# An encoder block on one core: a third seven-product K pair in the output projection, transposed halves in another sequence, token sums at other steps

## The chip, the cores and the metric

The kernel runs on one core of one Trainium2 chip. A core has five engines that run at once, each with its own in-order queue: TensorE (PE in the profile; PEld is its weight load), VectorE (DVE), ScalarE (ACT), GpSimd (POOL) and SyncE (SP), which here issues the loads. They share an on-chip memory (SBUF) and the accumulators of TensorE (PSUM). The metric is device time in microseconds from one launch, median of the runs; lower is better.

## The reference, cut to what matters

One layer of an encoder block in float32, 256 tokens of width 2048. What is computed:

```python
h = rms_norm(x, g_mix); proj = h @ w_in        # q, k, v of three mixers, and three gates
oa, ob, oc = mixer_a(...), mixer_b(...), mixer_c(..., mem)   # dilated windows, grouped-query, cross-attention
gates = sigmoid(gt).reshape(b, s, 3, D_MODEL)
merged = gates[:, :, 0] * (oa @ w_br_a) + gates[:, :, 1] * (ob @ w_br_b) + gates[:, :, 2] * (oc @ w_br_c)
x = x + merged @ w_o                           # "the projection" below
hf = rms_norm(x, g_ffn) @ w_ffn_in             # 2048 -> 2 x 5632
x = x + (silu(hf[..., :D_FF]) * hf[..., D_FF:]) @ w_ffn_out
```

## The kernel before, in words

**Split operands.** Each float32 operand is split into a high half, rounded by ScalarE (`whi` for weights, L397), and a low half, the rest, by VectorE (`wlo`, L407). A product of 128 rows by 512 columns is then three matmuls: high x high, high x low, low x high.

**Pairs and steps.** From the merging stage on, all matrix products run as pairs: two blocks of 512 output columns (c = 0, 1), two blocks of 128 tokens (t = 0, 1), and K in pairs of 128-row blocks (K pair u is blocks 2u and 2u+1). A whole K pair takes 8 products: step `d`u for column block 0 and step `D`u for column block 1, four products each, into the PSUM banks Y, V and Z, Q. A K pair can instead take seven products of summed operands, as Strassen and Winograd do: step `f`u (banks X, Y), step `g`u (W, Z), `h` (V, for up to two K pairs), `p` and `q` (X, for up to two K pairs each). Its weight sums are VectorE adds (L506, L507, L513, L529) and one transfer that adds while it loads, issued by POOL (L485); its token sums ("forms") are made by `token_sums` (L796 to L798 and a split, L130 and L131) from a full operand that VectorE (L807) or ScalarE (L301) puts together. The lists `STEPS_*` (L54 to L61) say in which order the steps of a pair run. In the projection's list two of the eight K pairs take seven products, in the first FFN list three, in the later ones four.

**What sets the order.** `run` keeps five steps in flight: a step's loads, sums and splits are written when it is reached, its matmuls four steps later. TensorE and SyncE keep the program's order; the weight splits and sums keep it among themselves (`follow`), and a low half is written one step after its high half (`low(1)`). Everything else on VectorE and ScalarE is placed by the compiler's planner, with `high_priority` for what is marked urgent. Each step that has been multiplied is a tick; `side` holds jobs that wait for a tick, and one of them advances at each tick. A number that a job yields is how many ticks it waits.

**Around the change.** When a column block of the projection ends, `add` adds it to the residual (L872), and its job `later` squares it (L878), waits 2 ticks, and calls `transposed`: two halves, two ticks apart, each with four transposes by TensorE into one PSUM bank, then a split with the gain into `x1T` (L133 on ScalarE, L134 on VectorE), which the FFN multiplies. For four of the eight halves ScalarE also copies the rows for the forms (L301). When an FFN pair ends, VectorE multiplies its two blocks (L924), and the result is transposed into `hT`, the operand of the output stage (`feeding`). There are three rounds of FFN pairs (four, four, three) and output pairs (two each); the last round's output lists are `STEPS_LAST` and `STEPS_LAST2`. At the head of each output stage `sums_of` makes one form from `hT`; it lies in a buffer of its own, `form`.

The times are those of the profile's execution: the projection's matmuls run from 580 to 670 us.

Of the kernel before, what the change touches and what calls it, by code (L numbers as in the profile page):

```python
# [11 lines left out]
F32 = mybir.dt.float32  # L12
F32R = mybir.dt.float32r
I32 = mybir.dt.int32
AF = mybir.ActivationFunctionType
ALU = mybir.AluOpType
# [3 lines left out]
S = 256  # L20
# [32 lines left out]

STEPS_GATE = "d4 d0 D0 f1 g1 d5 D5 f2 d6 g2 D4 f3 h1 g3 p0 p2 D6 q0 h3 q2 d7 D7".split()  # L54
STEPS_IN = "d0 D0 f1 d5 D5 g1 f2 g2 d6 h1 f3 f4 g3 D6 g4 p0 p2 h3 q0 q2 d7 D7".split()
STEPS_O = "d0 D0 d1 D1 f2 d4 g2 D4 f3 d5 g3 D5 h2 d6 p0 D6 q0 d7 D7".split()
STEPS_FFN = "d0 D0 d1 D1 f2 f3 d5 g2 D5 g3 h2 f4 d6 g4 p0 p2 h4 D6 q0 q2 d7 D7".split()
STEPS_OUT = "d3 d2 d1 f5 d0 D2 D1 f6 D0 g5 f7 D3 g6 g7 p0 p2 h5 q0 q2 h7 d4 D4".split()
STEPS_OUT2 = "d1 d2 d0 f5 D0 D2 g5 f6 f7 g6 g7 p0 d3 p2 D1 h5 h7 q0 D3 q2 d4 D4".split()
STEPS_LAST = "d1 d0 D0 D1 f2 g2 d4 D4 f3 g3 p0 h2 q0 d5 D5".split()  # L60
# [41 lines left out]
def encoder_block(ctx: ExitStack, tc: tile.TileContext, a: dict, out: bass.AP):  # L102
    nc = InOrder(tc)
# [16 lines left out]
    def s4(shape, name, dt=F32):  # L120
        return mid.tile(shape, dt, name=name, tag="s4")

    def bank(name, tag="at"):
        return psum.tile([P, NC], F32, name=name, tag=tag)


    def split(hi, lo, src, scale=None):

        if scale is None:
            nc.scalar.activation(hi, src, AF.Copy)  # L130
            nc.vector.tensor_sub(lo, src, hi.bitcast(F32))  # L131
        else:
            nc.scalar.activation(hi, src, AF.Copy, scale=scale)  # L133
            nc.vector.scalar_tensor_tensor(lo, src, scale, hi.bitcast(F32), op0=ALU.mult, op1=ALU.subtract)  # L134
# [145 lines left out]
    def transposed(src, dst, g=None, lag=1, also=None):  # L280


        for h in range(2):
            if h:
                yield lag
            tp = bank("tp", "mm" if h and nc.on else "at")
            for k in range(2):
                for t in range(T):
                    nc.tensor.transpose(tp[:, k * S + t * P:k * S + (t + 1) * P],
                                        src[t][:, (2 * h + k) * P:(2 * h + k + 1) * P], ident)  # L290
            if g is None:
                d = dst(2 * h, 2)
                split(d[0], d[1], tp.rearrange("p (k s) -> p k s", s=S))
            else:
                for k in range(2):
                    d = dst(2 * h + k, 1)
                    split(d[0], d[1], tp[:, k * S:(k + 1) * S], g(2 * h + k))
            if also and also(h):
                full = s4([P, 4, P], "ffull")
                for k in range(2):  # L300
                    nc.scalar.activation(full[:, 2 * k:2 * k + 2], tp[:, k * S:(k + 1) * S].rearrange(  # L301
                        "p (b s) -> p b s", s=P), AF.Copy, scale=g(2 * h + k) if g else 1.0)
                also(h)(full)
# [485 lines left out]
    mT, x1T, x = [], [], []  # L789
# [8 lines left out]
        nc.vector.tensor_add(raw[:, 3], raw[:, 2], full[:, 2])  # L798
        split(to[:, 0], to[:, 1], raw)

    def sums_of(lhs, these, room):

        def steps():
            for u, to in zip(these, room):
                full = s4([P, 4, P], "ffull")
                for k in range(2):
                    nc.vector.tensor_add(full[:, 2 * k:2 * k + 2].rearrange("p t s -> p (t s)"),  # L807
                                         *(v.bitcast(F32) for v in lhs(2 * u + k)))
                token_sums(full, to)
                yield 1  # L810
        start(steps())
        return by_pair(these, room)

    def by_pair(these, room):
        return lambda u, f: (room[these.index(u)][:, 0, (f + 1) % 4], room[these.index(u)][:, 1, (f + 1) % 4])

    def form_room(n, pool=None):
        tiles = [s8([P, 2, 2, 4, P], "forms", pool=pool) for _ in range((n + 1) // 2)]
        return [tiles[i // 2][:, i % 2] for i in range(2 * len(tiles))]

    form = lambda: spare[0].tile([P, 2, 4, P], F32R, name="form")

    def merging():
        forms = sums_of(xT, (1, 2, 3, 4), form_room(4, tail))
        for b, (g0, k0, k1) in enumerate(((0, 0, 2), (8, 2, 6), (4, 6, 12))):
            for j in (0, 2) if b else (2,):
                sg = [None, None]

                def gates(c, r, sg=sg):
                    sg[c] = r  # L830
                    for t in range(T):
                        nc.scalar.activation(r[:, t], r[:, t], AF.Sigmoid, scale=r_x[:, 0, t:t + 1])

                def merge(c, r, j=j, b=b, sg=sg):
                    n0 = (j + c) * NC
                    for t in range(T):
                        nc.vector.tensor_mul(sg[c][:, t] if b else mg[t][:, n0:n0 + NC], r[t], sg[c][:, t])

                    def later():
                        yield 1  # L840
                        for t in range(T):
                            m = mg[t][:, n0:n0 + NC]
                            nc.vector.tensor_add(m, m, sg[c][:, t])
                        if b == 2:
                            to = s8([P, 2, 4, S], "mT", pool=tail)
                            mT.append(to)
                            yield 2
                            yield from transposed([mg[t][:, n0:n0 + NC] for t in range(T)],
                                                  lambda k, n: (to[:, 0, k:k + n], to[:, 1, k:k + n]))
                    if b:  # L850
                        start(urgent(later()))

                yield pair(block_pair(a["w_gate"], g0 + j), xT, STEPS_IN if b else STEPS_GATE, gates, forms)
                yield pair(lambda u, c, j=j, k0=k0: a["w_br"][j + c][k0 // PK + u], lambda k, k0=k0: ol(k0 + k),
                           whole_k((k1 - k0) // 2), merge)

    x1l = lambda k: (x1T[k // 4][:, 0, k % 4], x1T[k // 4][:, 1, k % 4])
    forms, room = [], []


    def projecting():
        x.extend(s8([P, D], f"x{t}", F32) for t in range(T))
        for t in range(T):
            nc.sync.dma_start(out=x[t], in_=a["x"][t * P:(t + 1) * P, :])
        x1T.extend(s8([P, 2, 4, S], "x1T") for _ in range(4))
        mTl = lambda k: (mT[k // 4][:, 0, k % 4], mT[k // 4][:, 1, k % 4])
        oforms = sums_of(mTl, (2, 3), form_room(2))
        for n in (0, 2):
            def add(c, r, n=n):
                xc = [x[t][:, (n + c) * NC:(n + c + 1) * NC] for t in range(T)]  # L870
                for t in range(T):
                    nc.vector.tensor_add(xc[t], r[:, t], xc[t])  # L872

                def later():
                    yield 1
                    sq = s4([P, T, NC], "sq")
                    for t in range(T):
                        nc.scalar.activation(sq[:, t], xc[t], AF.Square, accum_out=ss1[:, t, n + c:n + c + 1])  # L878
                    yield 2
                    if n + c == 0:  # L880
                        room.extend(form_room(4) + [form()])
                        forms.append(by_pair((1, 2, 3, 4), room[:4]))

                    def token_forms(h):
                        u = 2 * (n + c) + h
                        return (lambda v: token_sums(v, room[u - 1])) if 1 <= u <= 4 else None
                    yield from transposed(xc, lambda k, m: (x1T[n + c][:, 0, k], x1T[n + c][:, 1, k]),
                                          lambda k: gT[:, 2, 4 * (n + c) + k:4 * (n + c) + k + 1], 2,
                                          also=token_forms)
                    if n + c == 3:  # L890
                        yield 2
                        ssr = small.tile([P, T], F32, name="ss", bufs=1)
                        nc.vector.tensor_reduce(ssr, ss1, axis=AX.X, op=ALU.add)
                        row_scale(ssr, r_f)
                start(urgent(later()))
            yield pair(block_pair(a["w_o"], n), mTl, STEPS_O, add, oforms)

# [5 lines left out]
    def feeding():  # L903
        for c0, c1 in ((0, 4), (4, 8), (8, KF // 4)):
            hT = []
            last = c1 == KF // 4
            hTl = lambda k, hT=hT: (hT[k // 4][:, 0, k % 4], hT[k // 4][:, 1, k % 4])
# [23 lines left out]
                           lambda u, f: forms[0](u, f))  # L931
            if last:
                pairs = STEPS_LAST, STEPS_LAST2
                sums_of(hTl, (1,), room[4:])
                out_forms = by_pair((1, 2, 3), room[4:] + late)
            else:
                pairs = STEPS_OUT, STEPS_OUT2
                sums_of(hTl, (5,), room[4:])
                out_forms = by_pair((5, 6, 7), room[4:] + late)
            for n in (0, 2):  # L940
                def output(c, r, n=n, last=last):
# [108 lines left out]
```

## Time and profile before

| What | Value |
|---|---|
| median of the runs | 1368.85 us |
| the profiled execution | 1369.74 us |
| its span, first to last instruction | 1368.0 us |
| instructions in all | 17866 |
| VectorE busy | 1190.5 us (87%) |
| ScalarE busy | 865.4 us (63%) |
| moved between HBM and the core | 298.86 MB |

TensorE's busy time is modelled from pipelined matmuls, so a busy TensorE may still hold short waits; they show in the start times of matmuls that follow each other. The profiled execution is one run; numbers of single instructions are its own, and its time is 0.89 us above the median.

### The profile page before, as it was taken

The page shows a single profiled execution, that of the slowest core. Times are in us where ns is not written, and L with a number is a line of the kernel's source. Part 1 is how long each engine was busy: PE and PEld are TensorE (multiplying, and loading weights), DVE is VectorE, ACT ScalarE, POOL GpSimd, SP SyncE. Part 2 cuts the span into 40 slices and gives each one's busy share as a digit, 9 for nine tenths or more (in the row PEclk, how much of TensorE's full clock was granted, in tenths as well). Part 3 has the DMA queues.
Part 4 walks back from the last instruction along what each step waited for, and adds up shares of the span by engine and source line. Part 5 has one row for each costly group of instructions (what it writes and reads, how often), then busy time and mean ns, then how long its engine had stood idle before and what let it go on. Part 6 is the DMA issues. An engine that isn't in the chain of part 4 may idle for free.

```text
span 1368.0 us, 17866 instructions
## 1 busy us (share of the span) xinstructions
PE 1358.7 (99%) x6195; PEld 1125.7 (82%) x6195; DVE 1190.5 (87%) x1652; ACT 865.4 (63%) x1152; POOL 85.1 (6%) x97
## 2 busy tenths in 40 slices
PE   9999999999999999999999999999999999999998
PEld 7888888888888888887878888888888888888887
DVE  6868877759889888878999998989999989899998
ACT  7777665646665565656776666655666765566754
POOL 0010000000000100000000010000001000011000
PEclk9999999999999999999999999999999999999999
DMA  9976445557776775954777777777787767787673
GB/s 366 343 234 203 151 156 168 171 166 225 239 237 201 225 242 180 308 181 146 242 223 220 233 211 221 220 246 212 222 247 218 230 187 243 217 247 225 204 224 108
DMA packets 91674, 298.86 MB, mean 218 GB/s; under 512 B 10368, under 2 KB 12928, under 8 KB 91328
## 3 DMA queue, kind: packets, MB, share of 16 engines
q1 hardware_dynamic: 79488, 275.94, 60.2%
q0 software_dynamic: 11952, 21.76, 9.7%
q8 instruction: 48, 0.79, 0.2%
q14 instruction: 42, 0.34, 0.1%
q10 hardware_dynamic: 144, 0.02, 0.0%
HBM read 294.81 MB, written 2.88 MB: 218 GB/s over the span
## 4 chain that ended last, share of the span: by engine, by line
PE 86%; DVE 8%; issue 2%; DMA 2%; ACT 1%; SPq 0%; DVEq 0%; ACTq 0%
PE mm L77 16%; PE mmZ L77 14%; PE mmV L77 14%; PE mmY L77 14%; PE mmQ L77 11%; PE mmX L77 10%; DVE wlo L407 4%; PE mmW L77 3%; DMA raw<-in_w_ffn 2%; PE tp L77 1%; ACT whi L397 1%; PE sc L77 1%; PE o L77 1%; DVE t L506 1%; PE pT L77 1%
## 5 line engine op out<-in xcount | busy, mean ns | idle before, releaser
L397 ACT ACTIVATE whi<-raw 128x1024 fp32r<-128x1024 f32 (+1 forms) x460 | 479.4, 1051 | 350.6 <-PE mmV L77 109.6
L407 DVE TENSOR_TENSOR wlo<-raw,whi 128x1024 fp32r<-128x1024 f32 (+1 forms) x460 | 546.8, 1210 | 80.7 <-ACT whi L397 77.5
L77 PE MATMUL mm<-whi,xT 128*128 128x512 f32 x640 | 202.5, 393 | 0.0
L131 DVE TENSOR_TENSOR wlo<-raw,whi 128x1024 fp32r<-128x1024 f32 x82 | 102.1, 1248 | 43.6 <-ACT whi L130 42.9
L77 PEld LDWEIGHTS mm<-whi,xT 128*128 128x128 f32 x640 | 119.3, 188 | 23.5 <-issue 0.4
L130 ACT ACTIVATE whi<-raw 128x1024 fp32r<-128x1024 f32 x82 | 86.7, 1061 | 62.3 <-PE mm L77 45.4
L77 PE MATMUL mm<-wlo,xT 128*128 128x512 f32 x320 | 125.7, 393 | 0.0
L407 DVE TENSOR_TENSOR wlo<-t,whi 128x1024 fp32r<-128x1024 f32 x90 | 102.2, 1138 | 13.4 <-ACT whi L397 12.9
L397 ACT ACTIVATE whi<-t 128x1024 fp32r<-128x1024 f32 x90 | 89.0, 990 | 25.5 <-PE mmQ L77 11.4
L77 PE MATMUL mmX<-whi,forms 128*128 128x512 f32 x312 | 104.9, 389 | 0.0
L77 PE MATMUL mmY<-whi,x1T 128*128 128x512 f32 x266 | 96.7, 394 | 0.8 <-DVE x1T L134 0.8
L77 PE MATMUL mmV<-whi,x1T 128*128 128x512 f32 x266 | 91.3, 390 | 0.0
L77 PEld LDWEIGHTS mm<-wlo,xT 128*128 128x128 f32 x320 | 60.2, 188 | 12.3 <-issue 0.7
L77 PEld LDWEIGHTS mmX<-whi,forms 128*128 128x128 f32 x312 | 58.6, 188 | 12.3 <-ACT SB L448 0.2
L485 POOL DMA_DIRECT2D raw<-in_w_ffn x43 | 37.2, 865 | 441.0 <-DMA raw<-in_w_ffn 143.3
L77 PE MATMUL mmZ<-whi,x1T 128*128 128x512 f32 x180 | 63.0, 391 | 0.0
L77 PE MATMUL mmQ<-whi,x1T 128*128 128x512 f32 x180 | 62.8, 390 | 0.0
L77 PE MATMUL mmW<-whi,forms 128*128 128x512 f32 x156 | 61.6, 395 | 0.0
L77 PE MATMUL mmZ<-whi,forms 128*128 128x512 f32 x156 | 60.9, 390 | 0.0
L77 PE MATMUL mmX<-wlo,forms 128*128 128x512 f32 x156 | 60.8, 389 | 0.0
L77 PEld LDWEIGHTS mmY<-whi,x1T 128*128 128x128 f32 x266 | 50.0, 188 | 11.3 <-DVE x1T L134 1.2
L507 DVE TENSOR_TENSOR t<-t,raw 128x512 f32<-128x512 f32 x83 | 57.1, 688 | 1.6
(285 smaller groups left out, 2837.9 us busy)
## 6 DMA issues: line engine op xcount, KB each, us to landing
raw<-in_w_ffn SPq DMA_DIRECT2D x176, 512.0 KB, 4.7
raw<-in_w_gate SPq DMA_DIRECT2D x96, 512.0 KB, 4.4
raw<-in_w_ffn_out SPq DMA_DIRECT2D x88, 512.0 KB, 4.6
raw<-in_w_qkv SPq DMA_DIRECT2D x64, 512.0 KB, 4.3
raw<-in_w_o SPq DMA_DIRECT2D x32, 512.0 KB, 4.8
raw<-in_w_br SPq DMA_DIRECT2D x24, 512.0 KB, 4.2
raw<-in_w_ffn POOLq DMA_DIRECT2D x43, 256.0 KB, 5.5
raw<-in_w_mem SPq DMA_DIRECT2D x15, 512.0 KB, 8.3
```

What stands on the lines that cost most here:

```text
L77: ins = op(*args, **kw)
L130: nc.scalar.activation(hi, src, AF.Copy)
L131: nc.vector.tensor_sub(lo, src, hi.bitcast(F32))
L397: nc.follow(nc.scalar.activation(hi[:, o], v, AF.Copy))
L407: nc.follow(nc.vector.tensor_sub(*due.pop(0)))
L485: nc.gpsimd.dma_start(out=b2[:, 0], in_=src(u, 0)[:, :NC], accum_op=ALU.add)
L506: nc.follow(nc.vector.tensor_add(s2, b2[:, 0], b2[:, 1]))
L507: nc.follow(nc.vector.tensor_sub(s3, s2, b1[:, 0]))
```

## The change

Four things change.

1. `STEPS_O`: K pair 1 of the projection, whole before, takes seven products too (f1, g1, h1), three of eight now, and the steps have another order. Its form is made in the merging stage, ahead of the last branch product, in the buffer `form` (`oroom`). `STEPS_FFN`, the list of the very first FFN pair, has g2 ahead of d5 and g3 ahead of D5.
2. `transposed`, where there is a gain: the two column halves of a transposed bank are split high, high, low, low, where they were high, low, high, low.
3. In `add`, the second block's job waits 3 ticks ahead of its transposes, the first block's 2, as before.
4. `sums_of` can wait some ticks: the form at the head of the output stage is begun 8 ticks later in the last round, 3 ticks later in the other two.

```diff
-STEPS_O = "d0 D0 d1 D1 f2 d4 g2 D4 f3 d5 g3 D5 h2 d6 p0 D6 q0 d7 D7".split()
-STEPS_FFN = "d0 D0 d1 D1 f2 f3 d5 g2 D5 g3 h2 f4 d6 g4 p0 p2 h4 D6 q0 q2 d7 D7".split()
+STEPS_O = "d0 D0 f1 d4 g1 D4 f2 g2 h1 d5 f3 D5 g3 d6 h3 p0 p2 D6 q0 q2 d7 D7".split()
+STEPS_FFN = "d0 D0 d1 D1 f2 f3 g2 d5 g3 D5 h2 f4 d6 g4 p0 p2 h4 D6 q0 q2 d7 D7".split()
...
             else:
+                d = [dst(2 * h + k, 1) for k in range(2)]
                 for k in range(2):
-                    d = dst(2 * h + k, 1)
-                    split(d[0], d[1], tp[:, k * S:(k + 1) * S], g(2 * h + k))
+                    nc.scalar.activation(d[k][0], tp[:, k * S:(k + 1) * S], AF.Copy, scale=g(2 * h + k))
+                for k in range(2):
+                    nc.vector.scalar_tensor_tensor(d[k][1], tp[:, k * S:(k + 1) * S], g(2 * h + k),
+                                                   d[k][0].bitcast(F32), op0=ALU.mult, op1=ALU.subtract)
...
-    def sums_of(lhs, these, room):
+    def sums_of(lhs, these, room, after=0):
 
         def steps():
+            if after:
+                yield after
             for u, to in zip(these, room):
...
+                if b == 2 and j == 2:
+                    oroom.append(form())
+                    sums_of(mTl, (1,), oroom)
...
-        oforms = sums_of(mTl, (2, 3), form_room(2))
+        oroom.extend(form_room(2))
+        sums_of(mTl, (2, 3), oroom[1:])
+        oforms = by_pair((1, 2, 3), oroom)
...
-                    yield 2
+                    yield 2 + c
...
-                sums_of(hTl, (1,), room[4:])
+                sums_of(hTl, (1,), room[4:], 8)
...
-                sums_of(hTl, (5,), room[4:])
+                sums_of(hTl, (5,), room[4:], 3)
```

More of the change, by code (lines that the diff above doesn't have):

```diff
@@ L819, in form_room @@
         return [tiles[i // 2][:, i % 2] for i in range(2 * len(tiles))]
+    mTl = lambda k: (mT[k // 4][:, 0, k % 4], mT[k // 4][:, 1, k % 4])
+    oroom = []
     form = lambda: spare[0].tile([P, 2, 4, P], F32R, name="form")
@@ L865, in projecting @@
         x1T.extend(s8([P, 2, 4, S], "x1T") for _ in range(4))
-        mTl = lambda k: (mT[k // 4][:, 0, k % 4], mT[k // 4][:, 1, k % 4])
-        oforms = sums_of(mTl, (2, 3), form_room(2))
+        oroom.extend(form_room(2))
+        sums_of(mTl, (2, 3), oroom[1:])
+        oforms = by_pair((1, 2, 3), oroom)
         for n in (0, 2):
```

## The prediction

> **What bounds the kernel now.** I read the page's busy times and chain first, then the chain around the projection, then the matmuls where it leaves TensorE, then group costs and stretches.
>
> ```profile
> PE 1358.7 (99%) x6195; PEld 1125.7 (82%) x6195; DVE 1190.5 (87%) x1652; ACT 865.4 (63%) x1152; POOL 85.1 (6%) x97
> PE 86%; DVE 8%; issue 2%; DMA 2%; ACT 1%; SPq 0%; DVEq 0%; ACTq 0%
> ```
>
> TensorE is the bound, and VectorE is the only other engine near it. So the change is worth the matmuls it removes, plus whatever it does to the few places where TensorE waits. The chain through the second projection pair, in order of time (start, us, what):
>
> ```profile
> 618.00 1.36 PE mmX L77 x6
> 634.02 1.06 ACT whi L397
> 635.08 0.74 ACT ffull L301 x2
> 635.84 0.42 DVE fraw L796
> 637.63 0.69 DVE t L506
> 638.96 1.23 DVE wlo L407
> 640.24 1.42 PE mmY L77 x5
> ```
>
> Six 512-column matmuls in 1.36 us are 0.227 us each; with the stream unbroken they follow each other at that pace. At 640.24 the chain comes from VectorE: a low half (wlo) was late because form sums and weight sums stood ahead of it. The matmul rows at the three stalls that the change touches:
>
> ```profile
> 638.56 0.63 PE L77 MATMUL mmY<-whi,mT 128*128 128x512 f32 x2
> 640.24 0.50 PE L77 MATMUL mmY<-wlo,mT 128*128 128x512 f32 x1 [1.04 <-DVE wlo L407]
> 640.57 0.62 PE L77 MATMUL mmY<-whi,mT 128*128 128x512 f32 x2
> 686.51 0.39 PE L77 MATMUL mmY<-wlo,x1T 128*128 128x512 f32 x1
> 687.69 0.50 PE L77 MATMUL mmY<-whi,x1T 128*128 128x512 f32 x1 [0.79 <-DVE x1T L134]
> 688.02 0.40 PE L77 MATMUL mmV<-whi,x1T 128*128 128x512 f32 x1
> 1307.53 0.39 PE L77 MATMUL mmQ<-whi,hT 128*128 128x512 f32 x1
> 1308.51 0.66 PE L77 MATMUL tp<-ident,SA 128*128 128x128 f32 x4 [0.59 <-DVE SA L924]
> ```
>
> At the 0.227 pace the matmul at 640.24 was due at 638.56 + 0.45 = 639.01, and the next came 0.33 later: 1.23 + 0.10 = 1.33 us lost. In the same way 687.69 was due at 686.74: 0.95 + 0.10 = 1.05 us. The transposes at 1308.51 were due at 1307.76: 0.75 us. These are the only stalls that edits here address: 3.13 us together.
>
> **The change part by part.** First the matmuls. A whole K pair is 8 products of 3 matmuls, 24; a seven-product one is 7 × 3 = 21. K pair 1 moves from one to the other in both column pairs of the projection: 2 × 3 = 6 fewer, 6 × 0.227 = **-1.36 us**. [...]
>
> What the seven products cost elsewhere comes from the groups (form kept apart: count, busy us, mean ns):
>
> ```profile
> L407 DVE TENSOR_TENSOR wlo<-raw,whi 128x1024 fp32r<-128x1024 f32 x451 | 540.7, 1220 | 78.9 <-ACT whi L397 75.7
> L407 DVE TENSOR_TENSOR wlo<-t,whi 128x512 fp32r<-128x512 f32 x14 | 9.6, 686 | 0.1
> L397 ACT ACTIVATE whi<-t 128x512 fp32r<-128x512 f32 x14 | 8.8, 626 | 3.9 <-PE mmQ L77 3.0 <-PE mmX L77 0.7 <-PE mmV L77 0.3
> L506 DVE TENSOR_TENSOR t<-raw 128x512 f32<-128x512 f32 x83 | 56.8, 685 | 0.0
> ```
>
> The old list has 19 steps, each one full high/low split. The new list has 22, of which 19 are full and 3 (h3, p2, q2) split 512 columns. So VectorE gains 3 × 0.686 = 2.06 us of low halves, and two weight sums (L506, L507) and one more sum at L529, all of L506's shape, 3 × 0.685 = 2.06: 4.1 us a pair, 8.2 us in all. ScalarE gains 3 × 0.626 = 1.9 us a pair; its share of the span is 63%, so I cost that at nothing while VectorE is the later of the two.
>
> Where VectorE can take it is read from stretches (length; busy of PE, PEld, DVE, ACT, POOL):
>
> ```profile
> 568.00:624.00 56.00, 56.00 (x257) 46.35 (x256) 42.80 (x50) 31.36 (x38) 2.59 (x3) 1.00 0.67 206
> 624.00:670.00 46.00, 44.96 (x206) 36.93 (x205) 39.72 (x56) 31.06 (x49) 1.73 (x2) 1.00 0.63 200
> 720.00:760.00 40.00, 40.00 (x182) 33.12 (x181) 37.83 (x43) 26.89 (x30) 2.93 (x4) 1.00 0.73 223
> 1299.00:1312.00 13.00, 12.41 (x58) 10.01 (x57) 13.00 (x17) 6.08 (x7) 0.62 (x1) 1.00 0.78 245
> 1312.00:1321.00 9.00, 9.00 (x43) 7.46 (x42) 7.11 (x8) 5.06 (x6) 1.10 (x2) 1.00 0.75 224
> ```
>
> Up to 624, about the first projection pair's stretch, VectorE is idle for 13.2 us: the added 4.1 vanish there, and if that cover were gone they would cost 4.1. In the second pair it is idle for 6.28 us. After the change that pair is 0.68 us shorter on TensorE, and 1.33 more if the stall goes, so 44.0 us long, with 39.72 + 4.1 = 43.8 us of VectorE work. That is as full as it can be, fuller than the FFN stretch at 37.83 of 40, which runs with TensorE busy throughout. What was VectorE idle for? The waits between 624 and 640 (waiter, releaser: total us, times, longest):
>
> ```profile
> DVE x1T L134 <- ACT x1T L133: 2.8, 3, 1.1
> DVE fraw L796 <- ACT ffull L301: 2.1, 1, 2.1
> ACT x1T L133 <- DVE x1T L134: 1.1, 2, 0.6
> ```
>
> 4.9 of the 6.28 us are hand-overs between ScalarE and VectorE on the transposed rows. They alternate: high half 0, low half 0, high half 1, low half 1, each waiting for the last. **The new sequence** (both high halves, then both low) has one crossing per transposed bank where it had three, and no added instruction. [...] `yield 2 + c` moves the second block's transposes from ticks 4 and 6 after the first block's end to 6 and 8 (at tick 5 the first block's second half takes the turn), and with them their PSUM reads on ScalarE and VectorE; nothing is queued past SyncE or POOL. So in this pair fewer hand-overs, in a more even order, against 4.1 us more work. Gain bounds: +1.33 (stall gone) to -2.7 (below, first rival). I take half the stall, **-0.7**: nearest is the FFN stretch, which has no stall at 95%, and this pair would be above it.
>
> The stall at 687.69 is named in its row: a low half of x1T that TensorE itself multiplies. The four banks' low halves ran as
>
> ```profile
> 675.76 0.47 DVE L134 SCALAR_TENSOR_TENSOR x1T<-tp,gT,x1T 128x256 fp32r<-128x256 f32 x1
> 678.75 0.87 DVE L134 SCALAR_TENSOR_TENSOR x1T<-tp,gT,x1T 128x256 fp32r<-128x256 f32 x2
> 682.36 0.87 DVE L134 SCALAR_TENSOR_TENSOR x1T<-tp,gT,x1T 128x256 fp32r<-128x256 f32 x2
> 686.76 0.87 DVE L134 SCALAR_TENSOR_TENSOR x1T<-tp,gT,x1T 128x256 fp32r<-128x256 f32 x2
> ```
>
> Each pair of them is the second half of one bank and the first of the next, as the alternation forces; the one wanted at 687.69 came a round (4.4 us) after its sibling. Grouped, both belong to the 682.36 round. Besides, the first block's bank now precedes the second block's, and STEPS_FFN puts g2 (6 matmuls, 1.36 us) ahead of d5, the reader. Any one of these covers 1.05 us. What is late next is g2's own low half, one step earlier than before: bounds +1.05 to -0.7 (two weight sums of 0.69 brought forward, half covered). I take **-0.95**.
>
> At 1308.51 TensorE waits for L924, and VectorE is busy without a gap before it (13.00 us of 13.00 from 1299); token sums for the output stage lie in that queue. Their pieces, the first row with least, median and most ns:
>
> ```profile
> L807 DVE TENSOR_TENSOR ffull<-hT x6: 417/418/421, 827.1 to 1288.3; 128x256 f32<-128x256 f32 x6
> L131 DVE TENSOR_TENSOR forms<-fraw,forms 128x512 fp32r<-128x512 f32 x16 | 10.9, 683 | 0.0
> L796 DVE TENSOR_TENSOR fraw<-ffull 128x256 f32<-128x256 f32 x19 | 8.0, 420 | 3.6 <-ACT ffull L301 3.5
> L798 DVE TENSOR_TENSOR fraw<-fraw,ffull 128x128 f32<-128x128 f32 x19 | 5.4, 286 | 0.1
> ```
>
> 2 × 0.418 + 0.42 + 2 × 0.286 + 0.683 = 2.5 us. Begun 8 ticks later they fall behind L924, into 1312 to 1321, where VectorE is idle for 9.00 - 7.11 = 1.9 us. Bounds: +0.75 (gone) to -0.6 (2.5 less the 1.9 of room). I take **-0.65**. The same sums started 3 ticks later in the two other output stages, where no row shows TensorE waiting on VectorE: nothing, as is the new 2.5 us for K pair 1 of the projection, begun in the last branch product (all whole steps; the 13.2 us of idle time cover it, and uncovered it costs 2.5). The form buffer it borrows is free again long before the output stage.
>
> Sum: 1.36 + 0.7 + 0.95 + 0.65 = 3.66. The profiled execution took 1369.74 us, its span 1368.0; the median of the runs is 1368.85, 0.89 below the profiled one. On the median the forecast is 1368.85 - 3.66 = **1365.2**.
>
> **The rivals.** *VectorE too full in the second pair (slower).* If the 4.9 us of hand-overs stay, only 6.28 - 4.9 = 1.4 us take the 4.1: short by 2.7, the old stall stays, and this pair's 0.68 of matmuls is lost behind VectorE: 1368.85 - 0.68 + 2.7 = 1370.9. It decides as soon as less than 2.7 us of hand-overs go. For it: 43.8 of 44.0. Against: x1T is not urgent in this pair, and operands are split some four steps ahead.
>
> *Only the matmuls go.* The instruction order on ScalarE and VectorE is the compiler's choice, and the new sequence may come out as the old interleaving, or each stall may reappear one step on: 1368.85 - 1.36 = 1367.5. So would the change not do what it says.
>
> *The summed weights come late.* g1 stands two places after f1, and needs a load, and an added load that POOL issues once the first has landed:
>
> ```profile
> raw<-in_w_o SPq DMA_DIRECT2D x32, 512.0 KB, 4.8
> raw<-in_w_ffn POOLq DMA_DIRECT2D x43, 256.0 KB, 5.5
> L485 POOL DMA_DIRECT2D raw<-in_w_o x4: 862/862/862, 562.6 to 617.8; - x4
> ```
>
> 4.8 + 0.86 + 5.5 = 11.2 us, against d0 D0 f1 d4 at TensorE's pace, 2.72 + 2.72 + 1.36 + 2.72 = 9.5. Without any lead 1.7 us are missing twice: 1365.2 + 3.4 = 1368.6, all of VectorE queued behind the waiting L506. Loads are asked for ahead of use, so I doubt it. [...]
>
> **How the numbers follow.** Forecast 0.55 (own range 1364.0 to 1366.6: all three stalls gone is 1368.85 - 1.36 - 3.13 = 1364.4, and I leave 0.4 for stalls elsewhere that shift); only the matmuls 0.20; VectorE too full 0.15; weights late 0.07; the rest unnamed. The range 1364.0 to 1369.4 takes in the second and fourth, and the milder half of the third (its 1370.9 with the 1.6 us of the other two stalls gained). Two per cent, about what a measurement of this kernel can tell from no change, is 27 us. No case here comes near it: 0.98 within, 0.01 on each side for what I don't see.
>
> **What would show it.** TensorE's count falls from 6195 to 6189. The row at 640 with a wait on wlo should be half as long; any wait on x1T after 686 gone; the transposes after the last FFN pair without a wait on L924. L134 rows should come in pairs of one bank, and the hand-over waits shrink below 2.2 us. Wrong I am if PE waits on wlo in both projection pairs, if L506 waits on a transfer, or if stalls appear after 1321, where the delayed token sums might push VectorE's last low halves.

## The result, and the profile after

The changed kernel takes 1375.93 us (median, 1374.86 to 1377.65), the kernel before 1368.84 us measured beside it. The ratio is 1.0058, with a 95% interval of 1.0047 to 1.0069: about 7 us **slower**, where 3.7 us faster was forecast. That is well within 2%, but above the forecast's range of 1364.0 to 1369.4 us. One execution of the kernel before took 1505.42 us; the ratios, here and below, leave such slow executions out. The profiled execution of the changed kernel took 1375.94 us, its span 1374.1 us.

The page of the changed kernel, busy times and then the chain's shares:

```profile
PE 1360.1 (99%) x6189; PEld 1124.7 (82%) x6189; DVE 1199.5 (87%) x1670; ACT 869.0 (63%) x1159; POOL 86.8 (6%) x99
PE 80%; DVE 13%; issue 3%; DMA 3%; ACT 1%; SPq 0%; DVEq 0%; ACTq 0%
```

TensorE has the six matmuls fewer that were forecast, yet VectorE's share of the chain rose from 8% to 13%: TensorE now waits for it more. The waits of TensorE in the changed kernel from 570 us to the end (waiter, releaser: total us, times, longest):

```profile
PE mmW L77 <- ACT forms L130: 3.5, 2, 1.7
PE mmW L77 <- DVE forms L131: 2.5, 2, 1.3
PE tp L77 <- DVE x L883: 1.1, 1, 1.1
PE tp L77 <- DVE SA L935: 0.6, 1, 0.6
```

The wait on `x1T` at 687 us is gone. The others that the forecast counted on are still there or have a successor: the wait on a low half (`wlo`) in the second projection pair gave way to one on the residual add (`x`, L872 before, L883 now), and the last product (L924, now L935) is as late as before. The first two lines are new and large: TensorE waits for `forms`, twice in ScalarE's half and twice in VectorE's. The matmul rows of the changed kernel show where:

```profile
867.09 0.39 PE L77 MATMUL mmZ<-whi,forms 128*128 128x512 f32 x1
869.20 0.50 PE L77 MATMUL mmW<-whi,forms 128*128 128x512 f32 x1 [1.73 <-ACT forms L130]
869.54 0.40 PE L77 MATMUL mmW<-wlo,forms 128*128 128x512 f32 x1
871.20 0.50 PE L77 MATMUL mmW<-whi,forms 128*128 128x512 f32 x1 [1.26 <-DVE forms L131]
...
1123.24 0.50 PE L77 MATMUL mmW<-whi,forms 128*128 128x512 f32 x1 [1.73 <-ACT forms L130]
1125.25 0.50 PE L77 MATMUL mmW<-whi,forms 128*128 128x512 f32 x1 [1.27 <-DVE forms L131]
...
1126.73 0.63 PE L77 MATMUL mmX<-whi,form 128*128 128x512 f32 x1
1127.15 0.63 PE L77 MATMUL mmX<-wlo,form 128*128 128x512 f32 x1
```

Both places are the output stages of the first two rounds, step g7. From start to start the two gaps at 867 are 2.11 and 1.66 us, where a matmul takes 0.227: 1.88 + 1.43 = 3.3 us lost, and the same again at 1121. After the second place some seven matmuls follow each other at 0.427 us instead of 0.227 (1126.73 to 1127.15 is one such step): some 1.5 us more. Together 3.3 + 3.3 + 1.5 = 8.1 us, in the profiled execution. Stretches of the changed kernel (length; busy of PE, PEld, DVE, ACT, POOL; granted clock; DMA share; GB/s) show what these slow matmuls are:

```profile
868.00:872.00 4.00, 1.53 (x5) 0.97 (x6) 3.15 (x4) 1.41 (x3) 0.00 (x0) 1.00 1.01 313
1125.00:1127.00 2.00, 1.75 (x5) 1.42 (x6) 0.19 (x1) 0.60 (x1) 0.00 (x0) 0.68 0.57 213
1127.00:1129.00 2.00, 2.00 (x6) 1.52 (x6) 0.69 (x1) 0.63 (x1) 0.00 (x0) 0.50 0.00 0
```

The granted clock falls to 0.50 after the second stall, not after the first, which is as long: there it was 1.00 from 868 to 872 us, and 1.00 from 872 to 874 us as well.

**Why the form is late.** It is the form of K pair 7, made from the second half of the last FFN pair's product in the round (the first half gives the form of K pair 6). In order of the program, TensorE transposes that half (`tp<-ident,SA`), ScalarE and VectorE put the rows and their sums together, then split them (L130, L131). In the kernel before, the rows of TensorE at these transposes and at step g7, and then the two halves of the form:

```profile
852.38 0.39 PE L77 MATMUL mmV<-whi,hT 128*128 128x512 f32 x1
852.61 0.60 PE L77 MATMUL tp<-ident,SA 128*128 128x128 f32 x4
...
869.41 0.39 PE L77 MATMUL mmW<-whi,forms 128*128 128x512 f32 x1
869.87 0.39 PE L77 MATMUL mmW<-whi,forms 128*128 128x512 f32 x1
```

```profile
866.18 0.62 ACT L130 ACTIVATE forms<-fraw 128x512 fp32r<-128x512 f32 x1
868.37 0.68 DVE L131 TENSOR_TENSOR forms<-fraw,forms 128x512 fp32r<-128x512 f32 x1
```

ScalarE's half ended at 866.80, 2.6 us ahead of step g7, which begins at 869.41. VectorE's half ended at 868.37 + 0.68 = 869.05. It is the third matmul of g7, at 869.87, that reads this half: a margin of about 0.8 us. And the rows of the changed kernel:

```profile
853.01 0.40 PE L77 MATMUL mmQ<-whi,hT 128*128 128x512 f32 x1
853.25 0.60 PE L77 MATMUL tp<-ident,SA 128*128 128x128 f32 x4
```

```profile
866.89 0.28 DVE L801 TENSOR_TENSOR fraw<-fraw,ffull 128x128 f32<-128x128 f32 x1
867.58 1.23 DVE L410 TENSOR_TENSOR wlo<-raw,whi 128x1024 fp32r<-128x1024 f32 x1 [0.41 <-ACT whi L400]
868.54 0.61 ACT L130 ACTIVATE forms<-fraw 128x512 fp32r<-128x512 f32 x1
868.73 1.22 DVE L410 TENSOR_TENSOR wlo<-t,whi 128x1024 fp32r<-128x1024 f32 x1
869.86 0.68 DVE L532 TENSOR_TENSOR raw<-t,raw 128x512 f32<-128x512 f32 x1
870.46 0.68 DVE L131 TENSOR_TENSOR forms<-fraw,forms 128x512 fp32r<-128x512 f32 x1
```

The transposes stood behind the matmuls of step d0, which end in bank V; now they stand behind those of D2, the next step, which end in bank Q. TensorE is by now 2.1 us earlier than in the kernel before: g7 is due at 867.31, 0.22 behind the matmul at 867.09. Measured against that, all of the form is late. Its last sum (L801) starts 0.4 us ahead of the time at which g7 is due, where it started 3.6 us ahead before (865.83). ScalarE's half ends at 869.15. Two low halves of weights and a weight sum stand between the last sum and VectorE's half, which ends at 871.14, where the third matmul was due at about 867.8.

What moved them is the order of turns. Every job in `side` that is due wants a tick, one job advances per tick, and **a job that ends uses up a turn as well**. The job of `sums_of` makes its sums in one turn, yields 1, and ends in the next. Delayed by 3 ticks, it makes the sums at tick 3 and ends at tick 4, and so takes the tick at which the job of the last FFN pair was due. That job's later turns, both its transposes among them, all come one tick, that is one step, later.

### The profile page after: what moved, and what is told of

It is laid out like the page before. It is cut to its first block, busy times and chain, and to the rows that moved or that the text cites. A ratio compares the mean times of both kernels' runs of the same rounds, so it can differ in the third digit from the quotient of the medians.

```text
span 1374.1 us, 17903 instructions
## 1 busy us (share of the span) xinstructions
PE 1360.1 (99%) x6189; PEld 1124.7 (82%) x6189; DVE 1199.5 (87%) x1670; ACT 869.0 (63%) x1159; POOL 86.8 (6%) x99
## 4 chain that ended last, share of the span: by engine, by line
PE 80%; DVE 13%; issue 3%; DMA 3%; ACT 1%; SPq 0%; DVEq 0%; ACTq 0%
PE mm L77 16%; PE mmV L77 13%; PE mmY L77 13%; PE mmZ L77 12%; PE mmX L77 10%; PE mmQ L77 9%; DVE wlo L410 8%; PE mmW L77 3%; DMA raw<-in_w_ffn 2%; ACT whi L400 1%; PE tp L77 1%; DVE t L509 1%; PE sc L77 1%; PE o L77 1%; DVE t L510 1%
## 5 line engine op out<-in xcount | busy, mean ns | idle before, releaser
L77 PE MATMUL mm<-whi,xT 128*128 128x512 f32 x640 | 202.3, 393 | 0.0
L131 DVE TENSOR_TENSOR wlo<-raw,whi 128x1024 fp32r<-128x1024 f32 x82 | 102.1, 1248 | 43.7 <-ACT whi L130 43.0
L77 PEld LDWEIGHTS mm<-whi,xT 128*128 128x128 f32 x640 | 119.2, 188 | 23.6 <-issue 0.4
L130 ACT ACTIVATE whi<-raw 128x1024 fp32r<-128x1024 f32 x82 | 86.7, 1061 | 61.8 <-PE mm L77 44.9
L77 PE MATMUL mm<-wlo,xT 128*128 128x512 f32 x320 | 125.6, 393 | 0.0
L77 PE MATMUL mmX<-whi,forms 128*128 128x512 f32 x312 | 105.3, 391 | 0.0
L77 PE MATMUL mmY<-whi,x1T 128*128 128x512 f32 x266 | 96.6, 392 | 0.0
L77 PE MATMUL mmV<-whi,x1T 128*128 128x512 f32 x266 | 91.3, 390 | 0.0
L77 PEld LDWEIGHTS mm<-wlo,xT 128*128 128x128 f32 x320 | 60.2, 188 | 12.4 <-issue 0.7
L77 PEld LDWEIGHTS mmX<-whi,forms 128*128 128x128 f32 x312 | 59.0, 189 | 12.5 <-ACT SB L451 0.2
L77 PE MATMUL mmW<-whi,forms 128*128 128x512 f32 x156 | 61.9, 397 | 6.0 <-ACT forms L130 3.5
L77 PE MATMUL mmZ<-whi,x1T 128*128 128x512 f32 x180 | 62.9, 390 | 0.0
L77 PE MATMUL mmQ<-whi,x1T 128*128 128x512 f32 x180 | 62.8, 390 | 0.0
L77 PE MATMUL mmZ<-whi,forms 128*128 128x512 f32 x156 | 61.1, 392 | 0.0
L77 PE MATMUL mmX<-wlo,forms 128*128 128x512 f32 x156 | 60.9, 391 | 0.0
L510 DVE TENSOR_TENSOR t<-t,raw 128x512 f32<-128x512 f32 x85 | 58.4, 687 | 1.5
L77 PEld LDWEIGHTS mmV<-whi,x1T 128*128 128x128 f32 x266 | 49.9, 188 | 10.5
```

The costliest lines, as they stand in the source:

```text
L77: ins = op(*args, **kw)
L510: nc.follow(nc.vector.tensor_sub(s3, s2, b1[:, 0]))
```

## The experiments

All times are medians with the ratio to the kernel before, measured on the same chip beside them. The kernel before took 1368.78 us beside e1 to e4, 1368.28 beside e5, e6, e7 and e9, and 1367.84 beside e8 and e10 to e12, so kernels of different groups are better compared by their ratios.

| Kernel | us | ratio [95%] | span |
|---|---|---|---|
| after | 1375.93 | 1.0058 [1.0047, 1.0069] | 1374.1 |
| e1, after without the 3 ticks | 1366.23 | 0.9984 [0.9975, 0.9994] | 1364.1 |
| e2, after, sums job ends in its first turn | 1366.02 | 0.9982 [0.9973, 0.9991] | 1363.7 |
| e3, before with the 3 ticks alone | 1378.68 | 1.0072 [1.0057, 1.0087] | 1375.4 |
| e4, after without the 8 ticks | 1374.98 (one time) | none | 1373.2 |
| e5, e1 with two seven-product pairs | 1365.58 | 0.9982 [0.9973, 0.9991] | 1363.1 |
| e6, e1 with high, low, high, low | 1367.85 | 0.9997 [0.9988, 1.0007] | 1365.7 |
| e7, e1 with `yield 2` | 1370.54 | 1.0013 [1.0004, 1.0023] | 1368.7 |
| e8, e1 with the old STEPS_FFN | 1365.85 | 0.9984 [0.9975, 0.9994] | 1364.0 |
| e9, e1 with `yield 3 + c` | 1365.34 | 0.9979 [0.9969, 0.9988] | 1363.4 |
| e10, before with the new sequence alone | 1366.50 | 0.9985 [0.9976, 0.9995] | 1365.0 |
| e11, before with the third seven-product pair alone | 1375.14 | 1.0054 [1.0037, 1.0071] | 1372.7 |
| e12, e10 with `yield 2 + c` | 1366.42 | 0.9987 [0.9977, 0.9996] | 1365.4 |

### The 3 ticks, taken out

The theory: the 3-tick delay costs the 8 us, by the turn that the ending job takes. The rival: the form is late because VectorE has more to do.

```diff
-                sums_of(hTl, (5,), room[4:], 3)
+                sums_of(hTl, (5,), room[4:])
```

> The changed kernel, with the 3-tick delay of the form in the first two output stages taken back. Delay theory (the two 3.3 us waits of TensorE on a form in those stages, and the half clock after the second, come from this delay): both waits go, 8 us less, 1367 to 1369 us. Rival, that the other edits brought these waits by shifting VectorE's work: they stay, 1375 to 1377 us.

Measured: 1366.23 us, ratio 0.9984. TensorE's waits from 570 us on:

```profile
PE tp L77 <- DVE x L883: 1.1, 1, 1.1
PE tp L77 <- DVE SA L935: 0.5, 1, 0.5
```

Both waits on `forms` are gone and the span is 10.0 us shorter than after's. Summing, in the two traces, how much later than at the pace of a running stream each matmul starts (0.227 us for 512 columns), 9.7 us of these are found: 3.9 between 850 and 951 us, 5.2 between 1110 and 1140, the rest in small pieces. So the 3 ticks cost about 10 us, and without them the change is faster than before.

### The 3 ticks kept, the turn given back

```diff
                 token_sums(full, to)
-                yield 1
+                if not after:
+                    yield 1
```

> The changed kernel, delays kept at 3 and 8 ticks, but a delayed sums job ends in the same turn in which it makes its form, where it took one more turn to end. Turns theory (the extra turn falls on the tick at which the last FFN pair's product wants its own, and so puts its transposes and the forms made from them one step later): the waits go as with no delay at all, 1367 to 1369 us. Rival, that the form made later loads VectorE at a worse place: the waits stay, 1375 to 1377 us.

Measured: 1366.02 us, ratio 0.9982, no wait on `forms`. The delays are the same; only the delayed jobs, the one with 8 ticks too, no longer take a second turn. The transposes of this kernel stand behind step d0 again, as in the kernel before:

```profile
849.76 0.40 PE L77 MATMUL mmV<-whi,hT 128*128 128x512 f32 x1
849.99 0.60 PE L77 MATMUL tp<-ident,SA 128*128 128x128 f32 x4
```

So it is not the lateness of the delayed sums, but the turn. That rules out the delayed work itself as the cause, and VectorE's load with it, since that load is the changed kernel's.

### The 3 ticks alone

The kernel before, with the parameter `after` and this call:

```diff
-                sums_of(hTl, (5,), room[4:])
+                sums_of(hTl, (5,), room[4:], 3)
```

> The kernel before, with the 3-tick delay alone. Delay theory: two waits on a form of about 3.3 us each in the first two output stages, 1375 to 1378 us (the clock may or may not drop after them, 1.5 us). Rival, that it takes the other edits' shift as well: within 1 us of before.

Measured: 1378.68 us, ratio 1.0072, 9.9 us slower than before. TensorE's waits from 840 to 1140 us, and a stretch behind the second stall:

```profile
PE mmW L77 <- ACT forms L130: 3.5, 2, 1.7
PE mmW L77 <- DVE forms L131: 2.5, 2, 1.2
```

```profile
1128.00:1130.00 2.00, 2.00 (x6) 1.57 (x5) 0.00 (x0) 1.11 (x2) 0.00 (x0) 0.50 0.07 27
```

The same stalls, without any other edit, to a tenth of a microsecond: nothing else of the change is needed for them. Again only the second one brings the half clock: the mean over the span is 0.999 of the full clock, as in the changed kernel.

### The 8 ticks, taken out

```diff
-                sums_of(hTl, (1,), room[4:], 8)
+                sums_of(hTl, (1,), room[4:])
```

> The changed kernel without the 8-tick delay in the last output stage. If the planner places these sums by when their operands are ready, not by the tick: nothing moves, the 0.73 us wait of the transposes on L924 stays with or without it, 1374 to 1378 us in one run. If the delay did hold them back: that wait changes by 0.3 us or more.

Measured: 1374.98 us, a single time, span 1373.2 against 1374.1. The wait on the last product is about the same with and without the 8 ticks (its row in this kernel: `PE tp L77 <- DVE SA L935: 0.5, 1, 0.5`, against 0.6 with them). So the delay does not relieve it. VectorE's rows show why: the low half of the delayed form starts 4.07 us ahead of the product in both kernels (1309.28 and 1313.35 with the 8 ticks, 1308.31 and 1312.38 without), so these sums did not move behind it. That wait is small and comes and goes with edits elsewhere: e2, e5, e7, e8 and e9 have the 8 ticks and not the wait, e10 and e12 do without the 8 ticks and have it. What sets it was not settled.

### The third seven-product pair, undone

The 3 ticks stay out from here on (e1 is the base).

```diff
-STEPS_O = "d0 D0 f1 d4 g1 D4 f2 g2 h1 d5 f3 D5 g3 d6 h3 p0 p2 D6 q0 q2 d7 D7".split()
+STEPS_O = "d0 D0 d1 D1 f2 d4 g2 D4 f3 d5 g3 D5 h2 d6 p0 D6 q0 d7 D7".split()
...
-                if b == 2 and j == 2:
-                    oroom.append(form())
-                    sums_of(mTl, (1,), oroom)
...
```

> e1 (the changed kernel without the 3-tick delay) with the projection's old list and without the form for K pair 1. Ledger theory: 6 matmuls more, +1.36 us, and the 1.33 us wait of the transposes on L883, which stands where the first list has weight sums ahead of the residual adds, goes: net 0, 1365.7 to 1366.8 us. Rival, that the wait on a low half of the kernel before comes back as well (1.33): 1367.0 to 1368.2 us. Rival, that VectorE's 8 us less work gives more than the matmuls took: under 1365.5 us.

Measured: 1365.58 us, ratio 0.9982; e1 with the third pair has 0.9984. The six matmuls come back, 1.36 us, and the time does not rise; the span is 1.0 us shorter. From 570 us on, no row of TensorE's waits is left. The second projection pair, without the third seven-product pair (e5) and with it (e1):

```profile
624.00:670.00 46.00, 46.00 (x212) 38.08 (x211) 41.01 (x59) 32.26 (x50) 2.60 (x3) 1.00 0.70 203
```

```profile
624.00:670.00 46.00, 44.87 (x206) 36.90 (x205) 43.99 (x63) 33.66 (x53) 3.45 (x4) 1.00 0.68 209
```

VectorE has 3.0 us more, TensorE 1.13 us of pause. Measured over 580 to 720 us, TensorE's late starts add up to 2.5 us in e5, 4.6 in e1 and 4.8 in the kernel before. So the third pair saves 1.36 us of matmuls and brings 2.1 us of waits, all of it in the projection: 1.3 us at the residual add (628 us in e1), and some 0.6 us at two transposes of the merged rows in the first pair (583 and 588 us), where the weight loads wait for VectorE's work on those rows; why that is late was not followed.

### The sequence of the halves, undone

```diff
-                for k in range(2):
-                    nc.scalar.activation(d[k][0], tp[:, k * S:(k + 1) * S], AF.Copy, scale=g(2 * h + k))
                 for k in range(2):
-                    nc.vector.scalar_tensor_tensor(d[k][1], tp[:, k * S:(k + 1) * S], g(2 * h + k),
-                                                   d[k][0].bitcast(F32), op0=ALU.mult, op1=ALU.subtract)
+                    d = dst(2 * h + k, 1)
+                    split(d[0], d[1], tp[:, k * S:(k + 1) * S], g(2 * h + k))
```

> e1 with the old sequence of the halves (high, low, high, low). If the sequence removed the 1.05 us wait of TensorE on x1T in the first FFN pair: that wait is back, 0.5 to 1.1 us, and VectorE's waits on ScalarE's x1T are back near 2.8 us, 1366.7 to 1367.5 us. Rival, that the moved g2 and the third tick covered it already: no wait on x1T, 1365.7 to 1366.7 us.

Measured: 1367.85 us, ratio 0.9997 against e1's 0.9984, span 1365.7 against 1364.1. So the sequence is worth some 1.6 to 1.8 us here; the two intervals overlap by a little. In its place a wait of the transposes on the last low half of the bank they need:

```profile
637.41 0.63 PE L77 MATMUL tp<-ident,x 128*128 128x128 f32 x4 [1.18 <-DVE x1T L134]
```

There is no wait on `x1T` by the FFN's matmuls in this kernel either, so the sequence was not needed for that one to go.

### The second block's wait: two ticks, three ticks

Of e1, in e7 and e9:

```diff
-                    yield 2 + c
+                    yield 2
```

> e1 with 2 ticks for both blocks. Order theory: the second block's first bank comes between the first block's two again; with grouped halves that costs no more than 0.4 us, 1365.8 to 1366.8 us, and the 1.33 us wait on L883 stays, since the first block's transposes are where they were. Rival, that the third tick is what removed the wait on x1T: it is back, 1366.8 to 1367.5 us.

```diff
-                    yield 2 + c
+                    yield 3 + c
```

> e1 with 3 ticks for the first block and 4 for the second. If the 1.33 us wait is only that the transposes stand one step too early for the residual adds: it goes, nothing else comes, 1364.6 to 1365.3 us, about 4 us under the kernel before. Rival, that VectorE is full in that pair and the wait only moves to a low half: 1365.8 to 1366.8 us.

Measured: e7 takes 1370.54 us, ratio 1.0013; e9 1365.34, ratio 0.9979. The third tick of the second block is worth about 4 us, far more than was expected. Without it (e7) TensorE's rows are

```profile
632.67 0.47 PE L77 MATMUL mmX<-whi,mT 128*128 128x512 f32 x1 [1.21 <-DVE x1T L299]
640.17 0.54 PE L77 MATMUL mmW<-whi,form 128*128 128x512 f32 x1 [2.23 <-DVE fraw L800]
640.52 0.63 PE L77 MATMUL mmW<-wlo,form 128*128 128x512 f32 x1
```

two waits that rows of this stretch put down to VectorE's work on the transposed rows and their sums. Neither matmul reads these; by the kernel's code (`bank`) the banks X and W come from the same turning sets of four as those of the transposes, so what they wait for is most likely a bank that has not been read out yet; no run tests this. There is the half clock behind the second (a granted clock of 0.52 from 642 to 644 us, 0.63 us a row again). In e9, where both blocks wait a tick more, the 1.1 us wait on the residual add is gone too, and the second pair of the projection is as full as can be without a pause:

```profile
624.00:670.00 46.00, 46.00 (x212) 38.06 (x212) 44.53 (x65) 34.32 (x54) 3.46 (x4) 1.00 0.69 216
```

VectorE is busy for 44.53 of 46 us here and TensorE does not stop. A full VectorE is not in itself what makes TensorE wait; what stands ahead of the urgent instruction is.

### The old first FFN list

```diff
-STEPS_FFN = "d0 D0 d1 D1 f2 f3 g2 d5 g3 D5 h2 f4 d6 g4 p0 p2 h4 D6 q0 q2 d7 D7".split()
+STEPS_FFN = "d0 D0 d1 D1 f2 f3 d5 g2 D5 g3 h2 f4 d6 g4 p0 p2 h4 D6 q0 q2 d7 D7".split()
```

> e1 with the old list of the first FFN pair (d5 ahead of g2, D5 ahead of g3). If the sequence of the halves or the third tick removed the 1.05 us wait on x1T by itself: no wait on x1T there, 1365.7 to 1366.8 us. If the moved g2 was needed: a wait on x1T near the start of that pair, 0.4 to 1.1 us, 1366.7 to 1367.4 us.

Measured: 1365.85 us, ratio 0.9984, as e1. No wait on `x1T` after 686 comes back. The earlier g2 and g3 bring nothing that shows when the sequence and the third tick are there.

### One part of the change alone

Three kernels add to the kernel before: e10 the sequence of the halves, e12 that and `yield 2 + c`, e11 the new STEPS_O with its form.

> The kernel before with the new sequence of the halves alone. Hand-over theory: both waits that stood behind the alternation go (1.33 us on a low half in the second projection pair, 1.05 us on x1T in the first FFN pair), 2.4 us under the kernel before, 1365.4 to 1366.4 us. Rival, that they need the third tick or the moved g2: 1366.8 to 1368.5 us, with one or both waits left.

> The kernel before with the new sequence and the third tick for the second block, nothing else. If the third tick matters only because of the third seven-product pair: as the sequence alone, within 0.5 us. If it helps by itself: 0.6 us or more below it. Either way no wait of TensorE over 0.4 us between 580 and 720 us, and about what the version with two seven-product pairs gave, 1365 to 1366 us.

> The kernel before with the third seven-product pair alone (its list, its form). Ledger of the prediction: 1.36 us less, whole if VectorE's 8 us more are covered, 1367.0 us. Fullness theory (VectorE is full in the second pair, and what it does late there are adds that TensorE's transposes wait for): new waits on L872 and on x1T of 3 to 6 us in that pair, 1370 to 1374 us.

Measured: e10 1366.50 us (0.9985), e12 1366.42 (0.9987), e11 1375.14 (1.0054). The sequence alone gives nearly all that e1 gives. The waits at 640 and 687 us are gone in e10; TensorE's waits from 570 us on are

```profile
PE mmZ L77 <- DVE wlo L410: 0.9, 1, 0.9
PE tp L77 <- DVE SA L927: 0.6, 1, 0.6
```

The tick changes nothing beside two seven-product pairs (e12), and 4 us beside three (e7). And the third pair alone costs 7.3 us, more than either theory had it. TensorE's and then VectorE's rows of e11:

```profile
631.24 0.60 PE L77 MATMUL tp<-ident,x 128*128 128x128 f32 x4
636.38 0.77 PE L77 MATMUL mmX<-whi,mT 128*128 128x512 f32 x1 [4.55 <-DVE x1T L134]
```

```profile
632.04 0.48 DVE L134 SCALAR_TENSOR_TENSOR x1T<-tp,gT,x1T 128x256 fp32r<-128x256 f32 x1
632.43 0.68 DVE L507 TENSOR_TENSOR t<-t,raw 128x512 f32<-128x512 f32 x1
...
635.37 0.87 DVE L134 SCALAR_TENSOR_TENSOR x1T<-tp,gT,x1T 128x256 fp32r<-128x256 f32 x2
```

This is the old alternation with the new load. The first low half of a transposed bank is made at 632.04; the second cannot be next, since ScalarE's second high half has to come between, and by then VectorE has taken up three sums and a low half of the weights, 2.94 us (632.43 to 635.37). TensorE waits 4.55 us for it at a matmul into `mmX` that does not read it, most likely again for a bank, which no run tests, and the half clock follows (0.50 from 637 to 640 us). So the sequence and the third tick are what makes the third pair bearable, and the third pair is what makes the tick worth anything: the parts do not add up one by one.

## Why the prediction was wrong, step by step

**The step that failed** is "The same sums started 3 ticks later in the two other output stages, where no row shows TensorE waiting on VectorE: nothing". It cost some 10 us (e1, e2, e3 agree). The work that was moved is 2.5 us on VectorE in each stage, and its own place hardly moved at all. In the kernel before, and then in the changed one, the sums at the head of the stage:

```profile
827.13 0.76 DVE L807 TENSOR_TENSOR ffull<-hT 128x256 f32<-128x256 f32 x2
```

```profile
826.11 0.75 DVE L812 TENSOR_TENSOR ffull<-hT 128x256 f32<-128x256 f32 x2
```

In e1, without the 3 ticks, they start at 826.21, which is no earlier. The planner places VectorE's work; the ticks decide the order in which jobs write theirs, and by it TensorE's order, since TensorE keeps the program's. The prediction costed the delayed instructions and not the queue of turns that they pass through. It says of `side` that one job advances at each tick, and does not ask who else was due at ticks 3 and 4. And "no row shows TensorE waiting" was read as room, where the margin was some 0.8 us.

**The matmuls, -1.36.** The count is right (6189), the gain is not there: e5 shows the third pair to be worth nothing or slightly less, since it brings 2.1 us of waits. The reason of the larger part is the rival's, VectorE too full in the second pair, in another form: not a low half that is late, but the residual add, behind the added weight sums. VectorE's rows of the changed kernel, and the same add in the kernel before:

```profile
625.35 0.68 DVE L510 TENSOR_TENSOR t<-t,raw 128x512 f32<-128x512 f32 x1
625.95 1.22 DVE L410 TENSOR_TENSOR wlo<-raw,whi 128x1024 fp32r<-128x1024 f32 x1
627.08 0.68 DVE L459 TENSOR_TENSOR SB<-mmQ,SB 128x512 f32<-128x512 f32 x1
627.68 0.68 DVE L883 TENSOR_TENSOR x<-SA,x 128x512 f32<-128x512 f32 x1
```

```profile
625.55 0.68 DVE L872 TENSOR_TENSOR x<-SA,x 128x512 f32<-128x512 f32 x1
```

The transposes at 627.02 need the add at 627.68. It starts 6.47 us after the block's first sum (`SA<-mmY`, at 621.21); in the kernel before that took 4.67 us (620.88 to 625.55). Two weight sums (L509 at 622.94, L510 at 625.35) and the sum at 627.08 are in front of it now and were not before, 0.60 us each; a low half like the one at 625.95 stood there before as well.

**The stall at 640, -0.7.** It is gone, but the one on the add (1.1 us by its row, 1.33 in start times) is as long. The forecast took half the stall for what would be left; it was a whole one, at another place. The new sequence is worth 1.3 to 2 us (e6, e10); the prediction took it only as cover for the added work. That it frees the 4.9 us of hand-overs is not shown: between 624 and 640 us VectorE has no wait on ScalarE's transposed rows left in e1, but none in e6 either, which has the old sequence and the same work, and e10, which has the new sequence without that work, still has 2.6 us of them on `x1T`.

**The wait at 687, -0.95.** Gone, as forecast, and with more cover than needed: e6, e7 and e8 each lack one of the three edits and have no such wait.

**The wait on L924, -0.65.** Nothing came of it: the 8 ticks did not place the sums behind the product (e4). It is the same error as the step that failed: ticks taken for places on VectorE, where these sums kept theirs.

Without the 3 ticks the change gives 1366.2 us, within the range and 1 us above the forecast. But the sum was not right for its reasons. Of the terms, only the wait at 687 came as told. Two waits on low halves at 948 and 1199 us, 0.5 us each in start times, went as well, and the forecast did not name them.

## What to carry to other kernels

Where jobs take turns, a job that is delayed also moves its last, empty turn: see whose turn that was, and which instruction on the engine with a fixed order moves with it. An engine without a wait may have a margin of less than a microsecond; before something is moved "at no cost", the margin of each operand that is made through the same queue is to be read from the trace. And where fewer operations on the bound engine buy more on the next one, look at what stands ahead of the urgent instruction there: with 44.5 of 46 us of VectorE busy TensorE went without a pause in one order (e9), and the same products cost 4 to 7 us in others (e7, e11).

## What was not expected of the hardware

A stall of TensorE can cost more than its length. After the stall of 867 to 871 us in the changed kernel the granted clock stayed 1.00 (868 to 874 us); after an equal one at 1121 to 1125 us it was 0.50 for 3.41 us (1125.73 to 1129.14), with a matmul every 0.427 us, and 1.5 us more were lost.

Stretches of e7 (the first two) and of e11:

```profile
640.00:642.00 2.00, 1.82 (x5) 1.49 (x6) 1.97 (x8) 1.12 (x4) 0.00 (x0) 0.62 1.03 414
642.00:644.00 2.00, 2.00 (x6) 1.53 (x6) 1.22 (x4) 1.47 (x3) 0.00 (x0) 0.52 0.51 209
632.00:637.00 5.00, 0.61 (x2) 0.55 (x3) 4.72 (x9) 1.84 (x5) 0.00 (x0) 0.85 0.41 131
637.00:640.00 3.00, 3.00 (x11) 2.41 (x10) 1.46 (x4) 1.86 (x4) 0.00 (x0) 0.50 0.00 0
640.00:643.00 3.00, 3.00 (x10) 2.40 (x10) 2.20 (x4) 1.30 (x3) 0.00 (x0) 0.61 0.11 11
```

If the clock was either 1.00 or 0.50 in them, it was at 0.50 for 2 × (2.00 × 0.38 + 2.00 × 0.48) = 3.4 us in e7 and for 2 × (5.00 × 0.15 + 3.00 × 0.50 + 3.00 × 0.39) = 6.8 us in e11: estimates, from these rows alone. By TensorE's rows the pauses that led to it were 1.73 and 1.27 us in the changed kernel, 2.23 us in e7 and 4.55 us in e11. The pauses at 867 to 871 us, 1.73 and 1.26, led to none. So what a pause costs by the clock does not follow from its length alone in these runs, and what decides it was not settled.
